# RMSNorm with SiLU on one core: one Sqrt and one reciprocal per two blocks, the gamma product in one instruction a block, and VectorE's program moved to a 128-instruction edge

## The chip, the core and the metric

The kernel runs on one core of one Trainium2 chip. The metric is device time of one launch in microseconds (us). The kernel before took 317.07 us, the median of three runs (316.85 to 317.13). A second number, the span, is read from a profiled execution: it goes from the first to the last instruction of the program.

## What is computed

```python
x: (8, 1024, 2048) float32, gamma: (2048,) float32, eps = 1e-5

rms = np.sqrt(np.mean(x ** 2, axis=-1, keepdims=True) + eps)
out = gamma * x / rms
return out * (1 / (1 + np.exp(-out)))        # SiLU of out
```

Input and output are 67.1 MB each. Every row of 2048 elements has a root mean square of its own.

## The kernel before, in words

The 8192 rows are cut into 16 blocks of 512 rows. A block gives each of the 128 partitions J = 4 whole rows, so it is a tile of 128 x 8192 float32, 4 MB, and one DMA moves it. A ring of BUFS = 6 such tiles (the tile `xt`) holds all blocks in flight: block b lives in slot b mod 6, is worked on in place, and block b + 6 may be loaded into the slot only when block b has been stored. Loads are issued by ScalarE (L67, and L71 for blocks 4 and 5 together, with 64 KB for each partition), stores by SyncE (L117). The DMA queue of the loads is q10 in the profile, that of the stores q1.

The steps of a block, with their lines:

- squares (L78 on ScalarE with Square, L86 on VectorE with a product that also sums): the sum of squares of each of the four rows, a column of the small tile `ss` each. `share(b)` says how many of the four rows ScalarE takes: one in blocks 4, 6, 8, 10 and 12, two in the others;
- `root` (L95, ScalarE): one Sqrt over the four sums;
- `invert` (L100, VectorE): one reciprocal of 128 x 4;
- `multiply` (L105, VectorE): for each row, x times the row's reciprocal times gamma, in one instruction a row;
- `silu` (L113, ScalarE): two instructions of two rows each;
- `store` (L117).

The last block goes another way: gamma alone is multiplied in (L177), and the reciprocal enters as the `scale` of four Silu instructions of one row each (L179).

Square, Sqrt and Silu are functions of ScalarE. Before the first Sqrt after a Silu, and before the first Silu after a Sqrt, the compiled program holds an ACT_TABLE_LOAD; Square needs none of its own.

The whole order is written out by hand (`manual_schedule`): each engine works through its own list in order, and the lists come from the loop at L145 to L171. For the first three blocks a block is multiplied, the squares of the next block follow on ScalarE, then its Silu. From block 3 on, the squares and the root of block b + 1 come before the product and Silu of block b. Loads 0 to 5 are issued at the start, loads 6 and 7 around the Silu of block 3, and load b + 3 after ScalarE's first row of squares of block b + 1. A load that has to wait for a store holds up ScalarE's list. gamma is spread over the partitions by eight matrix products at the start (L128) and copied to SBUF by VectorE (L130).

Of the kernel before, what the change touches and what calls it, by code (L numbers as in the profile page):

```python
# [1 line left out]

# [4 lines left out]

ACT = mybir.ActivationFunctionType
ALU = mybir.AluOpType


@with_exitstack
def kernel(
    ctx: ExitStack,
    tc: tile.TileContext,
    x: bass.AP,
    gamma: bass.AP,
    eps: bass.AP,
    out: bass.AP,
):  # L20

    nc = tc.nc
    P = nc.NUM_PARTITIONS
    f32 = mybir.dt.float32
    x2 = x.flatten_outer_dims()
    o2 = out.flatten_outer_dims()  # L30
    n, d = x2.shape
    J = 4
    BUFS = 6
    nblk = n // (P * J)
    PAIRS = (4,)

    def view(t, b):

        for q in PAIRS:
            if b in (q, q + 1):  # L40
                both = t[q * P * J:(q + 2) * P * J, :].rearrange("(p j) d -> p (j d)", p=P, j=2 * J)
                return both[:, (b - q) * J * d:(b - q + 1) * J * d]
        return t[b * P * J:(b + 1) * P * J, :].rearrange("(p j) d -> p (j d)", p=P, j=J)

    singles = ctx.enter_context(tc.tile_pool(name="singles", bufs=1))
    small = ctx.enter_context(tc.tile_pool(name="small", bufs=2))
    psum = ctx.enter_context(tc.tile_pool(name="psum", bufs=1, space=bass.MemoryType.PSUM))

    Q = 4
    w = d // Q  # L50
    g = singles.tile([P, d], f32)
    eps_t = singles.tile([P, 1], f32)
    ones = singles.tile([P, P], f32)
    junk_a = psum.tile([P, d], f32, name="junk_a")
    junk_v = psum.tile([P, d], f32, name="junk_v")
    ring = singles.tile([P, BUFS * J * d], f32, name="xt")
    sss, rmss, rstds = {}, {}, {}

    def rows(b, j, k):
        at = (b % BUFS) * J + j  # L60
        return ring[:, at * d:(at + k) * d]

    def row(b, j):
        return rows(b, j, 1)

    def load(b):
        nc.scalar.dma_start(out=rows(b, 0, J), in_=view(x2, b))  # L67

    def load_pair(b):
        both = x2[b * P * J:(b + 2) * P * J, :].rearrange("(p j) d -> p (j d)", p=P, j=2 * J)  # L70
        nc.scalar.dma_start(out=rows(b, 0, 2 * J), in_=both)  # L71

    def squares_scalar(b, loads=()):


        sss[b] = small.tile([P, J], f32, name="ss")
        for j in range(share(b)):
            nc.scalar.activation(out=junk_a, in_=row(b, j), func=ACT.Square,  # L78
                                 accum_out=sss[b][:, j:j + 1])
            if j == 0:  # L80
                for s in loads:
                    load(s)

    def squares_vector(b):
        for j in range(share(b), J):
            nc.vector.tensor_tensor_reduce(  # L86
                out=junk_v, in0=row(b, j), in1=row(b, j), scale=1.0, scalar=0.0,
                op0=ALU.mult, op1=ALU.add, accum_out=sss[b][:, j:j + 1])

    def share(b):  # L90
        return 1 if 4 <= b <= 12 and b % 2 == 0 else 2

    def root(b):
        rms = small.tile([P, J], f32, name="rms")
        nc.scalar.activation(out=rms, in_=sss.pop(b), func=ACT.Sqrt, scale=1.0 / d, bias=eps_t)  # L95
        rmss[b] = rms

    def invert(b):
        rstd = small.tile([P, J], f32, name="rstd")
        nc.vector.reciprocal(out=rstd, in_=rmss.pop(b))  # L100
        rstds[b] = rstd

    def multiply(b):
        for j in range(J):
            nc.vector.scalar_tensor_tensor(out=row(b, j), in0=row(b, j), scalar=rstds[b][:, j:j + 1],  # L105
                                           in1=g, op0=ALU.mult, op1=ALU.mult)

    def silu(b, between=()):
        for h in range(0, J, 2):
            if h:  # L110
                for s in between:
                    load(s)
            nc.scalar.activation(out=rows(b, h, 2), in_=rows(b, h, 2), func=ACT.Silu)  # L113
        store(b)

    def store(b):
        nc.sync.dma_start(out=view(o2, b), in_=rows(b, 0, J))  # L117

    with tc.manual_schedule():

        load(0)
        nc.vector.memset(ones, 1.0)  # L122
        nc.vector.memset(eps_t, float(eps))
        nc.scalar.activation(out=junk_a[:, 0:1], in_=ones[:, 0:1], func=ACT.Square)  # L124
        nc.sync.dma_start(out=g[0:1, :], in_=bass.AP(tensor=gamma.tensor, offset=gamma.offset, ap=[[d, 1], [1, d]]))
        for c in range(Q):
            cols = slice(c * w, (c + 1) * w)
            nc.tensor.matmul(junk_v[:, cols], ones[0:1, :], g[0:1, cols], start=True, stop=True)  # L128
        load(1)
        nc.vector.tensor_copy(out=g, in_=junk_v)  # L130
        nc.scalar.copy(out=junk_a[:, 0:1], in_=junk_v[:, d - 1:d])  # L131
        for b in range(2, PAIRS[0]):
            load(b)
        for b in PAIRS:
            load_pair(b)

        last = nblk - 1
        SOON = 3  # L140
        squares_scalar(0)
        squares_vector(0)
        root(0)
        invert(0)
        for b in range(last):  # L145
            loads = [b + 3] if BUFS + 2 <= b + 3 < nblk else []
            between = []
            if b + 3 == BUFS:

                load(BUFS)  # L150
                between = [BUFS + 1]
            if b < SOON:
                multiply(b)
                squares_scalar(b + 1, loads)
                silu(b)
                squares_vector(b + 1)
                root(b + 1)
            elif b < last - 1:
                squares_scalar(b + 1, loads)
                squares_vector(b + 1)  # L160
                root(b + 1)
                multiply(b)
                silu(b, between)
            else:
                multiply(b)
                squares_scalar(b + 1)
                silu(b)
                squares_vector(b + 1)
                root(b + 1)
            if b + 1 < last:  # L170
                invert(b + 1)  # L171


        for j in range(J):
            if j == J // 2:
                invert(last)
            nc.vector.tensor_mul(out=row(last, j), in0=row(last, j), in1=g)  # L177
        for j in range(J):
            nc.scalar.activation(out=row(last, j), in_=row(last, j), func=ACT.Silu,  # L179
                                 scale=rstds[last][:, j:j + 1])  # L180
        store(last)


# [1 line left out]
_INS = ['x', 'gamma', 'eps']  # L185
_OUTS = [((8, 1024, 2048), 'float32')]

_NUMBERS = {'eps': 9.999999747378752e-06}


# [26 lines left out]
```

## Time and profile before

| what | value |
|---|---|
| median of three runs | 317.07 us (316.85 to 317.13) |
| span of the profiled execution | 315.4 us |
| what the median has above that span | 1.6 us |
| moved by DMA | 134.24 MB, mean 426 GB/s over the span |
| VectorE (DVE) busy | 235.2 us, 75%, 157 instructions |
| ScalarE (ACT) busy | 212.5 us, 67%, 137 instructions |
| TensorE (PE) busy | 7.2 us, at the start |
| ACT_TABLE_LOAD | 31, of 1.28 us each |

The counts of instructions are of those that an engine itself executes. Waits for semaphores, drains and DMA issues are run by an engine's sequencer and are listed apart from them: in the trace VectorE's sequencer has 18 of those and ScalarE's has 40, so that the two programs are 175 and 177 instructions long as far as the trace holds them. The DMA row of the page gives the mean busy share of the core's 16 DMA engines in 40 slices of the span, and the queue lines give the packets of each queue; "instruction" packets are those that bring program code. The DMA of a 4 MB block falls into 128 packets of 32 KB, eight for each DMA engine.

### The profile page before, as it was taken

The page shows a single profiled execution, that of the slowest core. Times are in us where ns is not written, and L with a number is a line of the kernel's source. Part 1 is how long each engine was busy: PE and PEld are TensorE (multiplying, and loading weights), DVE is VectorE, ACT ScalarE, POOL GpSimd, SP SyncE. Part 2 cuts the span into 40 slices and gives each one's busy share as a digit, 9 for nine tenths or more (in the row PEclk, how much of TensorE's full clock was granted, in tenths as well). Part 3 has the DMA queues.
Part 4 walks back from the last instruction along what each step waited for, and adds up shares of the span by engine and source line. Part 5 has one row for each costly group of instructions (what it writes and reads, how often), then busy time and mean ns, then how long its engine had stood idle before and what let it go on. Part 6 is the DMA issues. An engine that isn't in the chain of part 4 may idle for free.

```text
span 315.4 us, 436 instructions
## 1 busy us (share of the span) xinstructions
PE 7.2 (2%) x8; PEld 2.5 (1%) x8; DVE 235.2 (75%) x157; ACT 212.5 (67%) x137; POOL 0.2 (0%) x4
## 2 busy tenths in 40 slices
PE   6300000000000000000000000000000000000000
PEld 2000000000000000000000000000000000000000
DVE  0679697944999999999693996939969399994000
ACT  1269998952289968993919849097591999999000
POOL 0000000000000000000000000000000000000000
DMA  8999999999999999999999999999999999999996
GB/s 333 411 453 411 386 532 399 399 440 424 428 437 424 437 432 432 432 432 440 424 440 424 445 420 457 407 457 407 465 399 465 399 465 399 465 403 461 411 453 270
DMA packets 4468, 134.24 MB, mean 426 GB/s; under 512 B 497, under 2 KB 497, under 8 KB 497
## 3 DMA queue, kind: packets, MB, share of 16 engines
q10 hardware_dynamic: 2160, 67.11, 49.6%
q1 hardware_dynamic: 2306, 67.12, 49.3%
q14 instruction: 2, 0.02, 0.0%
HBM read 67.12 MB, written 67.11 MB: 426 GB/s over the span
## 4 chain that ended last, share of the span: by engine, by line
DMA 55%; ACT 18%; DVE 14%; issue 2%; another core or an unknown queue 2%; ACTq 1%; DVEq 0%
DMA out_dram<-xt 40%; DMA xt<-in_x_dram 15%; ACT xt L113 9%; DVE xt L105 9%; DVE junk_v L86 5%; ACT junk_a L78 3%; ACT L95 2%; ACT xt L179 2%; ACT L113 1%; ACTq L212 1%; ACT rms L95 1%; ACTq L67 0%; ACT L179 0%; DVE rstd L100 0%
## 5 line engine op out<-in xcount | busy, mean ns | idle before, releaser
L105 DVE SCALAR_TENSOR_TENSOR xt<-xt,rstd,g 128x2048 f32<-128x2048 f32 x60 | 137.0, 2346 | 0.1
L113 ACT ACTIVATE xt<-xt 128x4096 f32<-128x4096 f32 x30 | 107.3, 3610 | 7.4 <-DVE xt L105 7.3
L86 DVE CUSTOM_DVE_ANT_0 junk_v<-xt 128x2048 f32<-128x2048 f32 x37 | 85.0, 2296 | 26.6 <-DMA xt<-in_x_dram 25.9
L78 ACT ACTIVATE junk_a<-xt 128x2048 f32<-128x2048 f32 x27 | 50.6, 1873 | 34.5 <-DMA out_dram<-xt 22.7
L95 ACT ACT_TABLE_LOAD x15 | 19.2, 1283 | 20.1 <-DMA out_dram<-xt 10.9
L113 ACT ACT_TABLE_LOAD x14 | 18.0, 1283 | 0.2
L100 DVE RECIPROCAL rstd<-rms 128x4 f32<-128x4 f32 x16 | 2.8, 174 | 15.0 <-ACT rms L95 15.0
L130 DVE COPY g<-junk_v 128x2048 f32<-128x2048 f32 x1 | 2.3, 2291 | 9.3 <-PE junk_v L128 9.3
L177 DVE TENSOR_TENSOR xt<-xt,g 128x2048 f32<-128x2048 f32 x4 | 8.9, 2278 | 0.0
L95 ACT ACTIVATE rms<-ss,eps_t 128x4 f32<-128x4 f32 x16 | 4.8, 297 | 5.5 <-DVE ss L86 5.3
L179 ACT ACTIVATE xt<-xt,rstd 128x2048 f32<-128x2048 f32 x4 | 7.7, 1990 | 0.0
L128 PE MATMUL junk_v<-g,ones 1*128 1x512 f32 x8 | 7.2, 1072 | 3.1 <-DMA g<-in_gamma_dram 3.1
L131 ACT COPY junk_a<-junk_v 128x1 f32<-128x1 f32 x1 | 0.1, 144 | 10.1 <-DVE g L130 10.1
L86 DVE DVE_READ_ACCUMULATOR2_ANT ss<- 128x1 f32 x37 | 5.2, 141 | 0.0
L78 ACT ACTIVATION_READ_ACCUMULATOR junk_a<-xt 128x1 f32 x27 | 5.0, 186 | 0.0
L128 PEld LDWEIGHTS junk_v<-g,ones 1*128 1x128 f32 x8 | 2.5, 325 | 6.2 <-issue 6.2
L124 ACT ACT_TABLE_LOAD x1 | 1.3, 1283 | 1.1 <-PEq L198 1.1
L179 ACT ACT_TABLE_LOAD x1 | 1.3, 1283 | 0.0
L122 DVE MEMSET ones<- 128x128 f32 x1 | 0.2, 165 | 0.8 <-PEq L198 0.8
L124 ACT ACTIVATE junk_a<-ones 128x1 f32<-128x1 f32 x1 | 0.2, 174 | 0.0
L198 POOL MEMSET const-bfloat16-1.0<- 128x1 bf16 x1 | 0.1, 103 | 0.0
L198 POOL MEMSET const-uint8-127<- 128x1 uint8 x1 | 0.1, 103 | 0.0
(3 smaller groups left out, 0.3 us busy)
## 6 DMA issues: line engine op xcount, KB each, us to landing
out_dram<-xt SPq DMA_DIRECT2D x16, 4096.0 KB, 39.1
xt<-in_x_dram ACTq DMA_DIRECT2D x14, 4096.0 KB, 26.6
g<-in_gamma_dram SPq DMA_DIRECT2D x1, 8.0 KB
xt<-in_x_dram ACTq DMA_DIRECT2D x1, 61.8
```

What stands on the lines that cost most here:

```text
L78: nc.scalar.activation(out=junk_a, in_=row(b, j), func=ACT.Square, accum_out=sss[b][:, j:j + 1])
L86: nc.vector.tensor_tensor_reduce(out=junk_v, in0=row(b, j), in1=row(b, j), scale=1.0, scalar=0.0, op0=ALU.mult, op1=ALU.add, accum_out=sss ...
L95: nc.scalar.activation(out=rms, in_=sss.pop(b), func=ACT.Sqrt, scale=1.0 / d, bias=eps_t)
L100: nc.vector.reciprocal(out=rstd, in_=rmss.pop(b))
L105: nc.vector.scalar_tensor_tensor(out=row(b, j), in0=row(b, j), scalar=rstds[b][:, j:j + 1], in1=g, op0=ALU.mult, op1=ALU.mult)
L113: nc.scalar.activation(out=rows(b, h, 2), in_=rows(b, h, 2), func=ACT.Silu)
L124: nc.scalar.activation(out=junk_a[:, 0:1], in_=ones[:, 0:1], func=ACT.Square)
L128: nc.tensor.matmul(junk_v[:, cols], ones[0:1, :], g[0:1, cols], start=True, stop=True)
L130: nc.vector.tensor_copy(out=g, in_=junk_v)
L177: nc.vector.tensor_mul(out=row(last, j), in0=row(last, j), in1=g)
L179: nc.scalar.activation(out=row(last, j), in_=row(last, j), func=ACT.Silu, scale=rstds[last][:, j:j + 1])
L212: with _tile.TileContext(nc) as tc:
```

## The change

- Blocks 0 and 1 stay as they were. From block 2 on blocks go in pairs (2 and 3, 4 and 5, ...): the eight sums of a pair share one `ss` tile, and there is one Sqrt of 128 x 8 and one reciprocal of 128 x 8 for the pair.
- From block 2 on `multiply` is one product of the whole block, 128 x 8192, with gamma repeated four times by its access pattern; the reciprocal is no part of it. It no longer waits for the root. `silu` is four instructions of one row each, with the row's reciprocal as `scale`, as the last block had it before.
- The order is written anew: the squares of b + 1, the root and the reciprocal of the pair, the product of b + 1, Silu of b, the squares and the product of b + 2, Silu of b + 1. Load 6 comes after the Silu of block 2, load 7 after ScalarE's squares of block 4.
- `addr_align(SLOTS, max_nops=0)` ahead of VectorE's first memset places what follows on an address that is a multiple of 128 instructions; what lies between is branched over.

```diff
+    SLOTS = 128
+    SINGLE = 2
+    SHARE = {4: 1, 6: 1, 8: 1, 10: 1, 12: 1}
...
+    def group(b):
+        return [b] if b < SINGLE else [b, b + 1]
+
+    def sums(b):
+        if b not in sss:
+            k = len(group(b))
+            t = small.tile([P, k * J], f32, name="ss")
+            for i, m in enumerate(group(b)):
+                sss[m] = (t, i * J)
+        return sss[b]
...
+    def plain(b):
+        return b >= SINGLE
+
     def root(b):
-        rms = small.tile([P, J], f32, name="rms")
-        nc.scalar.activation(out=rms, in_=sss.pop(b), func=ACT.Sqrt, scale=1.0 / d, bias=eps_t)
+        k = len(group(b)) * J
+        rms = small.tile([P, k], f32, name="rms")
+        nc.scalar.activation(out=rms, in_=sss[b][0], func=ACT.Sqrt, scale=1.0 / d, bias=eps_t)
         rmss[b] = rms
 
     def invert(b):
-        rstd = small.tile([P, J], f32, name="rstd")
+        k = len(group(b)) * J
+        rstd = small.tile([P, k], f32, name="rstd")
         nc.vector.reciprocal(out=rstd, in_=rmss.pop(b))
-        rstds[b] = rstd
+        for i, m in enumerate(group(b)):
+            rstds[m] = (rstd, i * J)
...
+    def scale(b, j):
+        t, at = rstds[b]
+        return t[:, at + j:at + j + 1]
+
     def multiply(b):
+        if plain(b):
+            whole = rows(b, 0, J).rearrange("p (j d) -> p j d", j=J)
+            nc.vector.tensor_mul(out=whole, in0=whole, in1=g.unsqueeze(1).to_broadcast([P, J, d]))
+            return
         for j in range(J):
...
-    def silu(b, between=()):
-        for h in range(0, J, 2):
-            if h:
-                for s in between:
-                    load(s)
-            nc.scalar.activation(out=rows(b, h, 2), in_=rows(b, h, 2), func=ACT.Silu)
+    def silu(b):
+        if plain(b):
+            for j in range(J):
+                nc.scalar.activation(out=row(b, j), in_=row(b, j), func=ACT.Silu, scale=scale(b, j))
+        else:
+            for h in range(0, J, 2):
+                nc.scalar.activation(out=rows(b, h, 2), in_=rows(b, h, 2), func=ACT.Silu)
         store(b)
...
         load(0)
+        nc.vector.addr_align(SLOTS, max_nops=0)
         nc.vector.memset(ones, 1.0)
...
+        multiply(1)
+        squares_scalar(2)
+        silu(1)
+        squares_vector(2)
+        multiply(2)
+
+        for b in range(SINGLE, nblk, 2):
+            squares_scalar(b + 1, [b + 3] if BUFS <= b + 1 and b + 3 < nblk else [])
+            squares_vector(b + 1)
+            root(b)
+            invert(b)
+            multiply(b + 1)
+            silu(b)
+            ahead = b + 2
+            if ahead < nblk:
+                if b == SINGLE:
+                    load(BUFS)
+                    silu(b + 1)
+                    squares_scalar(ahead, [BUFS + 1])
+                    squares_vector(ahead)
+                    multiply(ahead)
+                    continue
+                squares_scalar(ahead, [ahead + 2] if ahead + 2 < nblk else [])
+                squares_vector(ahead)
+                multiply(ahead)
+            silu(b + 1)
```

## The prediction

> **What bounds the kernel now.** I read the page first: busy shares, the DMA row, the queues, the groups.
>
> ```profile
> span 315.4 us, 436 instructions
> PE 7.2 (2%) x8; PEld 2.5 (1%) x8; DVE 235.2 (75%) x157; ACT 212.5 (67%) x137; POOL 0.2 (0%) x4
> ...
> DMA  8999999999999999999999999999999999999996
> ...
> q10 hardware_dynamic: 2160, 67.11, 49.6%
> q1 hardware_dynamic: 2306, 67.12, 49.3%
> q14 instruction: 2, 0.02, 0.0%
> ...
> L105 DVE SCALAR_TENSOR_TENSOR xt<-xt,rstd,g 128x2048 f32<-128x2048 f32 x60 | 137.0, 2346 | 0.1
> L113 ACT ACTIVATE xt<-xt 128x4096 f32<-128x4096 f32 x30 | 107.3, 3610 | 7.4 <-DVE xt L105 7.3
> L95 ACT ACT_TABLE_LOAD x15 | 19.2, 1283 | 20.1 <-DMA out_dram<-xt 10.9
> L100 DVE RECIPROCAL rstd<-rms 128x4 f32<-128x4 f32 x16 | 2.8, 174 | 15.0 <-ACT rms L95 15.0
> L177 DVE TENSOR_TENSOR xt<-xt,g 128x2048 f32<-128x2048 f32 x4 | 8.9, 2278 | 0.0
> L95 ACT ACTIVATE rms<-ss,eps_t 128x4 f32<-128x4 f32 x16 | 4.8, 297 | 5.5 <-DVE ss L86 5.3
> L179 ACT ACTIVATE xt<-xt,rstd 128x2048 f32<-128x2048 f32 x4 | 7.7, 1990 | 0.0
> ```
>
> No compute engine is over 75% busy; the DMA row is 9 in every slice but the first and last, and the two queues add to 98.9% of 16 engines' span. The kernel is bound by DMA. In the trace's packet records the usual 32 KB packet takes 1.213 us, whichever queue and whatever VectorE and ScalarE do beside it. A block is eight packets on each DMA engine, 8 x 1.213 = 9.70 us, and 32 transfers are 310.5 us of the 315.4. So work saved on VectorE or ScalarE counts for nothing unless it keeps the queues fuller or moves the last landing.
>
> Next I read the DMA view of the last 3.8 us, slice 0.095 us.
>
> ```profile
> DMA  7999799000000008000000000000000000000000
> GB/s 345 690 1035 1035 345 1380 690 0 0 0 0 0 0 0 0 345 0 0 0 0 0 0 0 0 0 0 0 0 0 0 0 0 0 0 0 0 0 0 0 0
> DMA packets 33, 0.56 MB, mean 147 GB/s; under 512 B 16, under 2 KB 16, under 8 KB 16
> ```
>
> Packets are drawn where they start. Sixteen 32 KB packets start by 312.2 us; a single one starts at 313.07. So 15 of the DMA engines are done by 313.39 and one alone works until 314.28: 0.89 us in which one engine of 16 holds the kernel. The landing records say since when. Between the second last and the last of a transfer's 16 completions there lie 0.05 to 0.13 us up to 94.8, and 0.83 to 0.92 in every transfer that lands after 106.9. What came between are the two instruction packets of q14, at 92.71 and 106.49 us, 8192 bytes and 0.309 us each, both on that engine. Against its neighbours it lost 0.43 us at the first (the store packet behind it took 1.333), 0.90 at the second (the load packet behind it took 1.747). It had been the first of the 16 to finish its packets, with a spread of 0.5 us, so the first delay was lost inside that spread.
>
> Whose packets they are I infer from the timelines around them.
>
> ```profile
> 91.69 3.62 ACT L113 ACTIVATE xt<-xt 128x4096 f32<-128x4096 f32 x1 [0.91 <-DVE xt L105]
> ...
> 105.29 0.17 DVE L100 RECIPROCAL rstd<-rms 128x4 f32<-128x4 f32 x1
> 105.38 2.27 DVE L86 CUSTOM_DVE_ANT_0 junk_v<-xt 128x2048 f32<-128x2048 f32 x1
> ```
>
> Counting sequencer rows, the ScalarE row is its 59th and the two VectorE rows its 61st and 62nd. Each releases a few more, and 1.0 to 1.1 us later a packet comes. Both programs are 175 to 177 long and would meet a block edge at the same count; VectorE is at its 53rd row at 92.7, ScalarE stands before its 70th at 106.5. So ScalarE's fetch is the first, VectorE's the second and dear one.
>
> **The change, part by part.**
>
> *VectorE's program.* Its 157 instructions become 37 squares, 37 accumulator reads, 8 row products of blocks 0 and 1, 14 block products, 9 reciprocals, 1 copy, 2 memsets: 108. With the 18 sequencer rows that is the 126 of the title, two under 128. I take a fetched packet of 8192 bytes to be one such block of 128: both programs meet one edge in 175 to 177, as they would. From an edge on, 126 need no second block. VectorE's fetch leaves the saturated stretch: 0.90 us off the late engine, of which 0.89 shows, since the other 15 end at 313.39. If the alignment moves the fetch to the entry at about 0.7 us, the packet comes near 1.8 us, where the loads begin (1.74): between nothing, because first packets are slowed unevenly there anyway (1.36 to 2.39 us), and one packet and its after-effect, 0.90. I take nothing to 0.3.
>
> *ScalarE's program.* Activations go from 78 to 97 (27 squares, 9 roots, 60 Silus, 1 warm-up), table loads from 31 to 19 (1 + 2 x 2 + 7 x 2), waits ahead of a root from 16 to 9: 177 + 19 - 12 - 7 = 177. So one fetch stays, near ScalarE's 60th row, which falls about 88 us in, among loads 6 and 7 and the stores of blocks 1 and 2. With a store packet behind it, it costs 0.43 (the first row), with a load packet 0.90. The cheap one ended inside the spread; I take it, since the store queue is full then, and keep 0.90, which would leave 0.06 + 0.90 - 0.49 = 0.47 us of lateness.
>
> The Trainium skill, "Runtime: NRT & Kernel Launch", section Instruction fetch mechanics, speaks against this gain: it calls the cost of crossing a block boundary "mostly hidden". By that rule the fetch would be worth nothing, and the sum 317.1. The trace agrees that no engine stalls at either fetch, and disagrees on the DMA side, where 0.9 us stays until the end.
>
> *Compute, off the path.* ScalarE: 12 table loads x 1.283 = 15.4 and 7 Sqrts x 0.297 = 2.1 us less; 56 row Silus at 7.7/4 = 1.92 are 107.8 against 26 x 3.58 + 7.7 = 100.7, so 7.1 more. VectorE: a block product is at most four row ones, 8.9 (L177), and saves three starts at best, some 0.2 us each; I take 8.7. A pair then costs VectorE five squares of 2.44 (L86's two rows), two products and a reciprocal, 29.8 us, and ScalarE 24.5, beside 38.8 us of DMA. It stays covered as long as the queues do not run dry, so I walk through the tightest places.
>
> *Block 2.* The product of block 1 ends at 46.26 as before, squares of block 2 at 50.9. Now its product comes next (to 59.6), squares of block 3 (64.4), table load and Sqrt (66.0), Silu's table load and four rows (75.0). Store 2 goes out at 75.0 instead of 65.65, load 6 at 75.0 instead of 66.83, and behind load 6 on ScalarE wait the Silu of block 3 and load 7. Eight transfers are queued by then; with all 32 done at 313.39 the eighth is done at 313.39 - 24 x 9.70 = 80.6. A store's first packet follows its issue by about 1 us, so 4.6 us are left. *Block 4.* Store 4 goes out near 109.3, twelve transfers last until 119.4. *The end.* All loads land by about 270. Blocks 14 and 15 now share a root: squares of block 15 to 275, Sqrt 276.5, Silu of block 14 to 285.5, of block 15 to 293 (281.3 and 291.6 before); the queue needs them by 294.0 and 303.7. All hidden. The cover is thinnest at block 2.
>
> Sum: 315.4 - 0.9 = 314.5 us of span. The median lies 1.6 above the profiled span, and the change touches nothing there: 317.07 - 0.89 = 316.2.
>
> **The rivals.**
>
> *The fetch gains little (same).* VectorE's fetch, moved to the start, costs the same engine 0.3 to 0.9 there, or ScalarE's falls ahead of a load packet (0.47 late), or I gave the packets to the wrong engines, and the one removed is the one of 0.43 (0.43 gained, 316.6). For it: two packets are few to price by. Against it: the store queue never empties around 88 us. Gain 0 to 0.6: 316.5 to 317.1. That the alignment does nothing is part of it: 317.1.
>
> *VectorE late at block 2 (slower).* If a block product with repeated gamma ran slower than four row ones, or VectorE started late behind the branch, both queues would be empty at 80.6 before store 2 and load 6 are out. Each us of lateness beyond 4.6 is one us of the total. Net of the 0.9 gained, it decides from 4.6 + 0.9 + 0.6 = 6.1 us: a product of 14.8 us or a start that much later. At 7.5 us the time is 317.07 - 0.89 + 2.9 = 319.1. If the product took twice its 8.7 us, a pair would need 47.2 us of VectorE against 38.8, and seven pairs some 59 more. Against it: the plain product runs at 2.28 us a row, and VectorE's first 2 us are covered, as TensorE waits for gamma until 3.1. For it: no row shows a repeated operand or a branch. The Trainium skill (same title and section) says that a branch out of the loaded window stalls for a fetch; no run here shows one.
>
> **How the numbers follow.** The three runs lie within 0.28 us of each other, so 0.2% (0.63 us) is about what a measurement can tell. The forecast, VectorE's fetch gone and ScalarE's lost in the spread, gets 0.53: 316.2, within 315.9 and 316.4 by the runs' own spread. The first rival gets 0.31, the second 0.16, most of it above 317.4. The range takes in forecast and first rival and leaves the second and a little below: 315.9 to 317.2.
>
> **What would show it.** One q14 packet of 8192 bytes left within the saturated stretch, near 88 us, or that one and another before 2 us. The last 32 KB packets of the 16 engines starting within 0.5 us, with no single one 0.9 later; the span 314.5. TENSOR_TENSOR of 128x8192 x14 near 8.7 us, 19 table loads, DVE x108. Store 2 at about 75 us with the DMA row at 9 through 80. Wrong, if two packets are left in the stretch, if the last engine is still late, or if the DMA row dips at 80, 119 or 294 us.

## The result: slower by 0.2%

The changed kernel takes 317.71 us in the median of 11 runs (317.27 to 318.15), the kernel before beside it 316.98 (316.78 to 317.44). The ratio is 1.002, with a 95% interval of 1.0012 to 1.0028. I had forecast 316.2 and a range up to 317.2.

The page of the changed kernel, with the lines that answer to those of before; the columns are the same.

```profile
span 315.3 us, 398 instructions
PE 7.2 (2%) x8; PEld 2.5 (1%) x8; DVE 229.3 (73%) x108; ACT 201.6 (64%) x144; POOL 0.2 (0%) x4
...
DMA  8999999999999999999999999999999999999996
...
q10 hardware_dynamic: 2160, 67.11, 49.7%
q1 hardware_dynamic: 2306, 67.12, 49.3%
q14 instruction: 2, 0.02, 0.0%
...
L130 DVE TENSOR_TENSOR xt<-xt,g 128x8192 f32<-128x8192 f32 x14 | 121.3, 8666 | 2.6 <-ACT junk_a L91 2.0
L139 ACT ACTIVATE xt<-xt,rstd 128x2048 f32<-128x2048 f32 x56 | 107.3, 1989 | 14.7 <-DMA out_dram<-xt 14.6
...
L119 DVE RECIPROCAL rstd<-rms 128x8 f32<-128x8 f32 (+1 forms) x9 | 1.8, 197 | 40.4 <-ACT rms L113 40.4
L113 ACT ACT_TABLE_LOAD x9 | 11.5, 1283 | 17.9 <-DVE ss L100 17.9
```

All the saved work is there: VectorE executes 108 instructions instead of 157, ScalarE is busy for 201.6 us instead of 212.5. The DMA row is as full as before and the span is as long. Two instruction packets are left in q14. The last 3.8 us of the DMA view, in slices of 0.095 us:

```profile
DMA  0999799000000700000000000000000000000000
GB/s 0 690 690 2070 345 690 1035 0 0 0 0 0 0 345 0 0 0 0 0 0 0 0 0 0 0 0 0 0 0 0 0 0 0 0 0 0 0 0 0 0
```

One 32 KB packet still starts alone, at 312.92 us; that engine ends at 314.13, the other 15 by 313.44. In this execution one engine of 16 holds the end for 0.70 us, where it was 0.89. VectorE's fetch did leave the middle of the kernel. It went to the start. The DMA view from 3.9 to 4.3 us, slice 0.01 us:

```profile
DMA  0900999900009000000000000000000000090000
GB/s 0 3277 0 0 819 3277 3277 3277 0 0 0 0 3277 0 0 0 0 0 0 0 0 0 0 0 0 0 0 0 0 0 0 0 0 0 0 3277 0 0 0 0
...
q10 hardware_dynamic: 6, 0.20, 121.9%
q14 instruction: 1, 0.01, 4.8%
```

The fifth slice is the 8 KB packet, at 3.948 us. The load packet that follows on its engine, in the thirty-sixth slice, takes 1.749 us instead of 1.213. Together they cost 0.307 + 1.749 - 1.213 = 0.84 us. In the records a packet starts within 5 ns of the end of the one ahead of it on its engine, so one engine can be followed by the times. The one that served this fetch finishes its part of the first load at 13.27 us, 0.79 behind the other 15, and it is the one that ends at 314.13.

That explains why the span did not shrink. It does not explain the slower time: 0.7 us of difference in the medians, and less than 0.1 in the mean spans (315.28 and 315.20). Each run gives its time and its span. Time minus span is 1.73 to 1.84 us in the runs of the kernel before (mean 1.79) and 2.29 to 2.41 in the changed kernel's (mean 2.33). The loss of 0.54 us lies outside the span, where no view of the profile reaches.

### The profile page after: what moved, and what is told of

Its sections match the earlier page's. It is cut to its first block, busy times and chain, and to the rows that moved or that the text cites. A ratio compares the mean times of both kernels' runs of the same rounds, so it can differ in the third digit from the quotient of the medians.

```text
span 315.3 us, 398 instructions
## 1 busy us (share of the span) xinstructions
PE 7.2 (2%) x8; PEld 2.5 (1%) x8; DVE 229.3 (73%) x108; ACT 201.6 (64%) x144; POOL 0.2 (0%) x4
## 4 chain that ended last, share of the span: by engine, by line
DMA 51%; ACT 21%; DVE 17%; issue 2%; ACTq 1%; DVEq 0%
DMA out_dram<-xt 44%; ACT xt L139 13%; DVE xt L130 8%; DMA xt<-in_x_dram 7%; DVE junk_v L100 6%; DVE xt L133 3%; ACT L113 2%; ACT junk_a L91 2%; ACT xt L142 2%; ACT L139 1%; ACTq L236 1%; ACT rms L113 0%; ACTq L70 0%; ACT L142 0%; DVE ss L100 0%
## 5 line engine op out<-in xcount | busy, mean ns | idle before, releaser
L130 DVE TENSOR_TENSOR xt<-xt,g 128x8192 f32<-128x8192 f32 x14 | 121.3, 8666 | 2.6 <-ACT junk_a L91 2.0
L139 ACT ACTIVATE xt<-xt,rstd 128x2048 f32<-128x2048 f32 x56 | 107.3, 1989 | 14.7 <-DMA out_dram<-xt 14.6
L119 DVE RECIPROCAL rstd<-rms 128x8 f32<-128x8 f32 (+1 forms) x9 | 1.8, 197 | 40.4 <-ACT rms L113 40.4
L133 DVE SCALAR_TENSOR_TENSOR xt<-xt,rstd,g 128x2048 f32<-128x2048 f32 x8 | 18.3, 2346 | 0.1
L142 ACT ACTIVATE xt<-xt 128x4096 f32<-128x4096 f32 x4 | 14.4, 3613 | 0.6 <-DVE xt L133 0.6
L113 ACT ACTIVATE rms<-ss,eps_t 128x8 f32<-128x8 f32 (+1 forms) x9 | 2.7, 300 | 0.1
```

The source lines that it names most:

```text
L113: nc.scalar.activation(out=rms, in_=sss[b][0], func=ACT.Sqrt, scale=1.0 / d, bias=eps_t)
L130: nc.vector.tensor_mul(out=whole, in0=whole, in1=g.unsqueeze(1).to_broadcast([P, J, d]))
L139: nc.scalar.activation(out=row(b, j), in_=row(b, j), func=ACT.Silu, scale=scale(b, j))
```

## The experiments

**First question: the alignment, or the rest?** Theory A put the loss on the alignment, theory B on the pairs and block products. Four kernels tell them apart. An edge is the end of one block of 128 instructions and the start of the next; a slot is the place of one instruction in a block.

The changed kernel without the alignment:

```diff
-        nc.vector.addr_align(SLOTS, max_nops=0)
```

> The changed kernel without the alignment. Theory A (the alignment adds some 0.7 us outside the span, and puts VectorE's instruction fetch at a moment where it costs its DMA engine 0.84 us): time minus span falls from 2.4 back to 1.6 us; VectorE's fetch returns to its 60th row, near 95 us, with a store packet behind it (0.43 us), like ScalarE's; two such leave 0.06 + 0.86 - 0.49 = 0.43 us of lateness on one engine: 316.5 us. Theory B (what lies outside the span grew with the rest of the change, the pairs and block products): time minus span stays at 2.4 us, 317.2 to 317.7 us.

Measured: 316.98 us (316.72 to 317.26), ratio 1.0 (0.9992 to 1.0009); mean span 315.04, time minus span 1.93. The whole loss is the alignment's. But the rest brings nothing either: 0.16 us less span, 0.14 more outside it. A's 1.6 us was too low (it set a median against the span of one execution; the mean over the runs is 1.79), its direction right. The last 3.8 us:

```profile
DMA  9799790007070000000000000000000000000000
GB/s 690 345 1380 690 345 1380 0 0 0 345 0 345 0 0 0 0 0 0 0 0 0 0 0 0 0 0 0 0 0 0 0 0 0 0 0 0 0 0 0 0
```

Two packets start late, in slices 10 and 12, and the last ends 0.21 us behind the one before it. The earlier one is on the engine that served VectorE's fetch; it ends at 313.68. The engine that ends last, at 313.89, served no fetch: followed back, it carries two slow load packets, of 2.456 us at 37.6 and 1.556 at 40.1, around the start of the first store. ScalarE's fetch fell on an engine that ends at 313.38, among the rest. Both fetches (103.6 and 120.6 us) have store packets behind them and cost 0.42 (ScalarE's) and 0.66 (VectorE's).

The kernel before with the alignment alone:

```diff
         load(0)
+        nc.vector.addr_align(128, max_nops=0)
         nc.vector.memset(ones, 1.0)
```

> The kernel before with the alignment alone. Theory A: time minus span 2.4 instead of 1.6 us; VectorE's 175 instructions now meet two edges, at the start (fetch near 4 us, 0.84 us) and 128 rows later (near 220 us, 0.4 to 0.9 us), beside ScalarE's one near 92 us: three fetches, 0.4 to 0.9 us more span; 318.0 to 318.6 us. Theory B: time minus span 1.6 us, two or three fetches, 317.0 to 317.6 us.

Measured: 317.51 us (317.21 to 318.12), ratio 1.0019 (1.001 to 1.0027). The three fetches came as expected (3.94, 92.72 and 215.85 us; 0.84, 0.42 and 0.66), and the span grew by 0.57 to 315.77. Both of VectorE's went through the same DMA engine, which ends 1.14 us behind the rest. The second came while VectorE ran its 131st row; the first row behind the edge is its 4th, so edges are some 128 instructions apart. But time minus span is 1.80. The same branch to the same edge costs nothing outside here, so theory A is wrong in that half.

The program placed within the block that it is in, behind a branch:

```diff
-        nc.vector.addr_align(SLOTS, max_nops=0)
+        nc.vector.addr_align(SLOTS, offset=100, max_nops=0)
```

> The changed kernel, VectorE's program placed at slot 100 of the block that it is in already, again with a branch over the padding, so the branch is there but leads to no new block. The edge comes after 28 rows, near 40 us. If the branch itself costs time outside the span: 2.4 us between time and span, as with the edge. If it is the jump to the next block: 1.6 us. The span: a fetch near 40 us, among the first stores, 0.43 to 0.9 us; total 316.5 to 317.0 us without the outside part, 317.3 to 317.8 us with it.

Measured: 316.98 us (316.72 to 318.44), ratio 1.0004 (0.9995 to 1.0013); time minus span 1.93, as without the alignment. A branch alone costs nothing outside. VectorE's fetch came at 56.4 us, at its 32nd row (28 behind slot 100), and cost 0.67 us with a store behind it.

No branch, the padding run through:

```diff
-        nc.vector.addr_align(SLOTS, max_nops=0)
+        nc.vector.addr_align(SLOTS, max_nops=SLOTS)
```

> The changed kernel at the same edge, the padding filled with no-operations that VectorE's sequencer runs instead of a branch. If the branch costs the time outside the span: 1.6 us between time and span. If the place of the program costs it: 2.4 us. Some 60 no-operations delay VectorE's first memset, by up to 3 us at 50 ns each, which the queues cover (4.6 us at block 2). The fetch comes near 4 us either way, with a load packet behind it: span 315.2 to 315.5 us; total 316.9 or 317.7 us.

Measured: 317.52 us (317.05 to 317.89), ratio 1.0018 (1.0009 to 1.0027); time minus span 2.28 without any branch, so the place costs it. The trace holds 61 no-operations, 47 ns apart, and the first memset moved from 1.39 to 4.10 us without the DMA row showing it. The fetch moved with it, to 7.27 us, and cost 0.84 again. The 61 also tell where the edge is: 61 slots behind the start barrier.

**Second question: where does the loss outside the span come from?** The edge at the start costs 0.4 us in a program of 124 instructions and nothing in one of 176. So I looked at the other end. Counted from that edge, VectorE's program in the changed kernel ends 7 slots before the next one (124 instructions, of which three lie ahead of the edge: 128 - 121), in the kernel before 16 (175, of which 63 lie ahead of it: 128 - 112), in the aligned kernel before 83 (176, three ahead: 256 - 173). Theory C: a program that ends a few slots before an edge costs time behind the span. Theory D: the start at the edge does, in the short program. ScalarE's program had grown too, from 177 to 182 instructions, and the small extra of 0.14 us in every kernel with 182 might be its end.

Three runs meant to lengthen programs by no-operations:

```diff
+        for _ in range(12):            # 9 on VectorE, 5 on ScalarE in the other two
+            nc.vector.nop(nofuse=True)
```

> The changed kernel with twelve no-operations at the end of VectorE's program, so that it meets the next edge within the kernel, while the last stores run, and ends some 5 slots behind an edge instead of some 7 before it. Theory C (a program that ends a few slots before an edge costs time behind the span, because what the runtime runs after it crosses the edge at once): time minus span falls from 2.33 to 1.93 us, as without the alignment. Theory D (the start at the edge costs it): stays 2.33. Both: a third fetch, near 280 us, with store packets behind it (0.43 to 0.66 us), so the span grows from 315.28 by 0 to 0.6. Total by C 317.2 to 317.8, by D 317.6 to 318.2 us.

> The kernel before with nine no-operations at the end of VectorE's program: it starts where it did and ends some 8 slots before an edge instead of 17. Theory C: time minus span grows from 1.78 to 2.2 or 2.3 us at an unchanged span of 315.2: 317.4 to 317.5 us. Theory D: 1.78 and 316.99 us.

> The kernel before with five no-operations at the end of ScalarE's program, which is then 182 instructions long, as in the changed kernel, instead of 177. Theory C: time minus span grows from 1.78 to 1.93 us, as in the changed kernel without the alignment; 317.1 us. Rival (the 0.15 us come from the pairs and block products themselves): 1.78 and 316.99 us.

They tell nothing between C and D: the traces hold no such instruction, the counts are those of the originals, so the no-operations had been dropped in the build. They are second looks at known programs: 317.89 us and 2.33 outside for the changed kernel, 316.99 and 316.98 us and 1.79 for the kernel before. The two further profiles of the kernel before are of use for the forecast's 0.89 (below).

The changed kernel without the alignment, and ScalarE's program shorter by ten:

```diff
-    SHARE = {4: 1, 6: 1, 8: 1, 10: 1, 12: 1}
+    SHARE = {b: 1 for b in range(4, 14)}
...
-        nc.vector.addr_align(SLOTS, max_nops=0)
```

> The changed kernel without the alignment, and with one row of squares on ScalarE instead of two in blocks 5, 7, 9, 11 and 13: ScalarE's program is ten instructions shorter (172), VectorE's ten longer. Theory C: no program ends near an edge, time minus span 1.75 to 1.80 us instead of 1.93; two fetches with store packets behind them as without the alignment, span 315.0: 316.8 us, 0.1 to 0.2 under the kernel before. Rival: VectorE's five added squares of 2.44 us (32.2 us a pair beside 38.8) let the queues run dry at the start of a pair: span 315.5 or more.

Measured: 316.77 us (316.56 to 317.3), ratio 0.9993 (0.9984 to 1.0002); span 315.03, time minus span 1.79. The 0.14 us are gone, as C says, and VectorE's longer list did not cost span. It is the fastest of all kernels here, and its interval still touches no change.

Then the programs were lengthened by instructions that stay. Twelve memsets behind the changed kernel:

```diff
+        for _ in range(12):
+            nc.vector.memset(ones[:, 0:1], 1.0)
```

> The changed kernel with twelve memsets of one column at the end of VectorE's program (the no-operations of the run before this were dropped when the program was built). VectorE now runs 136 instructions and meets the next edge within the kernel, after its last product, and ends some 5 slots behind an edge. Theory C (an end a few slots before an edge costs time behind the span): time minus span 1.93 instead of 2.33 us. Theory D (the start at the edge costs it): 2.33. Both: a third fetch near 285 us with a store packet behind it, 0.43 to 0.66 us on one engine, span 315.3 to 315.9.

Measured: time minus span 1.94 in a kernel that still starts at the edge. D is wrong. The time is 317.9 us all the same (317.65 to 318.28), ratio 1.003 (1.002 to 1.0039), for the span went to 316.02: there is a third fetch, and it went through the same DMA engine as the one at the start. The DMA view from 273 to 275 us, and the page's line of the memsets:

```profile
q1 hardware_dynamic: 44, 0.98, 115.3%
q14 instruction: 1, 0.01, 1.0%
```

```profile
L208 DVE MEMSET ones<- 128x1 f32 x12 | 0.7, 59 | 0.7
```

The packet came at 273.9 us, with a store packet of 1.567 behind it (0.66 us). I had expected it near 285, when VectorE reaches the edge; why it came at its 117th instruction, 14 slots before the edge, is open.

Nine memsets behind the kernel before, so that VectorE's program ends 7 slots before an edge without any alignment (the same edit with `range(9)`):

> The kernel before with nine memsets of one column at the end of VectorE's program: 184 instructions instead of 175, so that it ends at the same slot of a block as the changed kernel's does, some 7 before the edge, without any alignment. Theory C: time minus span 2.2 instead of 1.79 us, span as before (315.2), 317.4 us. Theory D: 1.79, 316.99 us.

Measured: 317.3 us (317.1 to 317.45), ratio 1.0008 (1.0 to 1.0016). Its timeline from 284 to 290 us and its page:

```profile
286.89 1.09 DVE L183 MEMSET ones<- 128x1 f32 x9
```

```profile
span 315.2 us, 445 instructions
```

The memsets are done 26 us before the last store lands, and the mean span is 315.13, 0.07 under the kernel before. Time minus span rose from 1.79 to 2.15. So 0.36 us come from nine instructions that no critical path holds, by where they let the program end: the twelve memsets of the run above, which let it end elsewhere, added none of it.

Five copies behind ScalarE's list in the kernel before:

```diff
+        for _ in range(5):
+            nc.scalar.copy(out=junk_a[:, 0:1], in_=ones[:, 0:1])
```

> The kernel before with five copies of one column at the end of ScalarE's program: 182 instructions as in the changed kernel. Theory C: time minus span 1.93 instead of 1.79 us, 317.1 us. Rival (the pairs and block products cost the 0.15 us): 1.79, 316.99 us.

Measured: 317.04 us (316.93 to 317.34), ratio 1.0001 (0.9993 to 1.001), span 315.12, time minus span 1.93, as C says. The 0.14 us are ScalarE's length, not the pairs. Whether they too come from an edge isn't shown: ScalarE's fetch came at its 59th row in the kernel before and at its 66th in the changed one, so its rows don't place the edge.

All together, means over the runs, in us:

| kernel | VectorE: length, slots left to an edge at its end | ScalarE length | span | time minus span |
|---|---|---|---|---|
| before | 175, 16 | 177 | 315.20 | 1.79 |
| before, aligned | 176, 83 | 177 | 315.77 | 1.80 |
| before, 9 memsets | 184, 7 | 177 | 315.13 | 2.15 |
| before, 5 copies | 175, 16 | 182 | 315.12 | 1.93 |
| changed | 124, 7 | 182 | 315.28 | 2.33 |
| changed, no-operations ahead | 184, 7 | 182 | 315.22 | 2.28 |
| changed, not aligned | 123, 68 | 182 | 315.04 | 1.93 |
| changed, at slot 100 | 124, 35 | 182 | 315.21 | 1.93 |
| changed, 12 memsets | 136, 123 | 182 | 316.02 | 1.94 |
| changed, not aligned, ScalarE shorter | 133, 58 | 172 | 315.03 | 1.79 |

The last column has two causes that add up: VectorE ending 7 slots before an edge, 0.36 us, and ScalarE's 182 instructions, 0.14; 1.79 + 0.36 + 0.14 = 2.29, measured 2.28 and 2.33. Between 7 and 16 slots nothing was measured. That what runs behind the program crosses the edge there is an inference; no view shows it. The Trainium skill, "Runtime: NRT & Kernel Launch", section The ~15µs preamble/postamble breakdown, lists work that the runtime does behind a kernel, a barrier and a reset of semaphores among it; no run here shows it.

## Why the prediction was wrong

**The bound and the cover were right.** The DMA row is full throughout, and the walk held to the last stage: store 2 went out at 75.8 us (75.0 forecast), store 4 at 109.3 (109.3), stores 14 and 15 at 285.3 and 292.8 (285.5 and 293). The timeline around block 2:

```profile
66.90 8.64 DVE L130 TENSOR_TENSOR xt<-xt,g 128x8192 f32<-128x8192 f32 x1
...
69.97 7.67 ACT L139 ACTIVATE xt<-xt,rstd 128x2048 f32<-128x2048 f32 x4
75.77 0.33 SPq L146 DMA_DIRECT2D out_dram<-xt  x1
```

The block product takes 8.67 us (8.7 taken), repeated gamma costs nothing, and the start was late by 0.56 us (first memset at 1.39 instead of 0.83). The slower rival did not come true; the kernel is slower for another reason. One reading of the cover was wrong: I took about 1 us from a store's issue to its first packet. Store 0, with no other store ahead of it, took 4.2 us in the kernel before (35.29 to 39.45) and 4.7 in the changed one. With 4.2 the cover at block 2 would have been 1.4 us and not 4.6.

**The term that failed in the span: the fetch at the start.** I took nothing to 0.3 us for it, and named 0.90 as its upper end. It cost 0.84. By the packets alone VectorE's fetch had cost the same before: 0.309 + 1.747 - 1.213 = 0.84. It was moved and not removed. ScalarE's fetch came at 102.4 us and not near 88, at its 66th row and not the 60th, which is open; with a store packet of 1.329 behind it, it cost 0.43 us, the price that I took. Here I had also misread the records: the two packets of the kernel before were not "both on that engine". Followed engine by engine, ScalarE's fell on one that was early among the 16, and was absorbed there; VectorE's fell on the one that was last already, and made up the lateness by itself: the first ends at 313.39 us, the second at 314.28. In every profile here the engine of ScalarE's fetch ends by 313.6, among the rest. This half is the first rival, "VectorE's fetch gains little". By that alone the time would have been 317.0.

**The term that was too large: the 0.89 to be had.** It was read from one execution with a span of 315.4, above the mean of 315.20. In two more profiles of the same program the last engine ends 0.07 and 0.26 us behind the second last, at spans of 315.2 and 315.3. The kernel before with nine memsets or five copies at its end gives 0.46 twice. In all five executions the last engine is the one that served VectorE's fetch, and the mean of the five is 0.43 and not 0.89. In the first of the two further profiles the last 3.8 us have two late packets where the prediction's had one:

```profile
DMA  7099999900007700000000000000000000000000
```

This one is of the kernel before in the run that was to be lengthened on VectorE. VectorE's engine ends at 314.06 us; the one that ends at 313.99 served no fetch. Followed back, it holds a load packet of 2.834 us at 37.67, around the start of the first store, where the longest in the prediction's profile is 1.966. The second last engine of the other profile (313.88) has one of 2.787 at 37.64. Why one engine is held there in some executions is open. With it close behind, less could be gained than I took. Taking the alignment out, with two fetches at 0.42 and 0.66, gave 0.16 us of span.

**The step that failed outside the span.** "The median lies 1.6 above the profiled span, and the change touches nothing there." It does, by 0.54 us, and that is nearly all of the loss of 0.63 between the means (317.62 and 316.99). I had counted VectorE's 126 instructions as fitting "two under 128" and took that for the merit of it; ending so near the edge, 7 slots by the trace, is the cost. For ScalarE I counted 177 instructions again, with seven waits fewer; the trace holds 182, for only two of its 22 sequencer waits went away. A count exact to five instructions seemed without weight, and was worth 0.14 us.

**The rule of "mostly hidden".** The Trainium skill, "Runtime: NRT & Kernel Launch", section Instruction fetch mechanics, calls the cost of crossing a block boundary "mostly hidden"; by that the alignment would be worth nothing. On the engines in the stretch of loads and stores the trace agrees: in the kernel before, VectorE's row that runs at 106.49 us ends at 107.66, and the next starts at 107.57. At the start it differs, for with the no-operations 0.52 us pass at the edge, from the last of them (3.58) to the first memset (4.10). It differs on the DMA side too, for a fetch costs 0.42 to 0.91 us on one DMA engine of 16 in every profile.

## What to carry to other kernels

When DMA is full from end to end, count what holds the last of the 16 DMA engines, and price it over several profiles: one late engine in one execution may be a draw. Alignment moved a fetch here and did not remove it, and a fetch cost less ahead of a store packet than ahead of a load packet. Look at time minus span before and after a change in the length of any engine's program; it may move when nothing in the profile does.

## What the runs showed of the hardware

An 8 KB instruction packet takes 0.307 to 0.309 us on its DMA engine (0.426 once, at the start of the kernel with twelve memsets) and delays what stands behind it, by the kind: store packets behind it took 1.326 to 1.333 or 1.564 to 1.569 us instead of 1.213, load packets directly behind it, or behind one 9 ns completion write, 1.696 to 1.751. The whole cost is 0.42 to 0.67 us before a store and 0.84 to 0.91 before a load, over the profiles named here, with one case between (0.55 before a load, in the kernel with ScalarE shorter). VectorE's and ScalarE's fetches load two different DMA engines of the 16 in every profile, so their costs do not add at the end; two fetches of VectorE's load the same one, and do.

A single load packet of 2.46 to 2.84 us, beside 1.97 at most in the first profile of the kernel before, starts between 37.6 and 39.0 us, around the start of the first store, in five of the 13 profiles. In four of the five it is on an engine that ends last or second last without having served a fetch.

Time outside the span depends on where VectorE's program ends and on how long ScalarE's is: 0.36 us for VectorE's end 7 slots before an edge rather than 16, 0.14 us for 182 instructions on ScalarE rather than 177, both at mean spans within 0.1 us of the kernel before.
